# Normed rows as two fp16 parts and two more ring slots in an encoder layer with experts

## The chip, the cores and the metric

The kernel runs on one core of a Trainium2 chip. The metric is the device time of one execution in microseconds, the median of the runs. The core has five engines that are told apart here: PE (TensorE, matmuls; its weight loads are PEld), DVE (VectorE), ACT (ScalarE), POOL (GpSimd) and SP (SyncE), which issues most DMAs. A program line is written L123.

## The reference, cut to what matters

One layer for 512 tokens of 1024 features: three attention branches, gated and merged, a layer norm, then 16 experts, each of which picks its 64 best tokens, and a second layer norm. The expert part:

```
logits = x @ w_router;  aff = softmax(logits)               # (512, 16)
gate, idx = top_k(aff.T, 64)                                # each expert picks 64 tokens
xs = x[idx]                                                 # (16, 64, 1024)
h  = xs @ w_gate_up                                         # (16, 64, 2048), weights (16, 1024, 2048)
ye = (silu(h[..., :1024]) * h[..., 1024:]) @ w_down         # weights (16, 1024, 1024)
ffn = zeros.at[idx].add(ye * gate)
x = layer_norm(alpha * x + ffn)
```

Everything is float32. The expert weights are 16 x 12 MB, read once.

## The kernel before

**First half: attention.** 74 weight units of 128x1024 numbers come over the SP queue into `raw` (two buffers, tag "raw"; units 2 to 9 go in pairs into halves of larger tiles). `hi_lo` splits each one into a high part (ACT, L84) and a rest (DVE, L85), so that three matmuls give nearly the precision of float32. The high part rotates over three buffers of the tag "hi", the rest over two of "lo" and one of "lo2". Softmax results use two buffers each of the tags "P" and "PT". An order written by hand interleaves attention units (`Attn.step`) with the projections.

**Routing.** The last products (`w_half`, L991) use `mh` and `ml` (buffers G0a to G1b). Beside them the rows are normed (`x1_norm`): the normed row times X_SCALE is kept as a high part `XH` (4 bytes, buffers A5 and A6) and a rest `XL` (fp16, buffer A8, written by POOL at L960). DVE finds the threshold of each expert (`rounds`), and PE counts positions with `tri_t` (buffer VS) at L1081 and L1084; `pos` tells which slot a token takes.

**Experts.** They go in quarters of four. `onehot(qd)` compares positions with slot numbers on DVE (L1100) into a 4-byte one-hot matrix, and ACT casts it to fp16 (L1103). `gather(qd)` multiplies: for each of 8 column blocks, four matmuls of `XH` with the 4-byte one-hot (L1113) and four of `XL` with the fp16 one (L1115); then `aff2`, the affinities in two parts, is gathered into `gw` (L1130, L1135). `gate_up(e, ks)` needs one load per k, 128 rows of the gate/up weights (L1149), `down(e)` four loads per expert (L1182). `act_h` lies between them, `h_transpose` and `slots_T` turn operands, and `combine` adds expert pairs back into the token rows. The last expert's down product is done by column quarters (`last_down`, `product`, L1297), followed by the second norm and the stores.

**The ring.** All 192 expert loads, 1 MB each (8 KB a partition), stand in one fixed order in `Ring`: the first four gate/up loads of an expert, the four down loads of the expert before, the other four gate/up loads; at the end the down loads of the last two experts. The buffers are those that earlier stages leave:

```
RING = ("E0", "A2", "A3", "A0", "A1", "B0", "B1", "P", "PT", "A4", "raw", "G0a", "G0b", "A7", "G1a", "G1b", "lo", "Ma", "Mb",
        "X")
ONCE = ("G1a", "G1b", "lo")
PAIRED = {"raw": ("raw", "raw"), "P": ("P", "P"), "PT": ("PT", "PT"), "lo": ("lo", "lo"), "X": ("VS", "lo2")}
N_EARLY = 11
```

Buffers of `ONCE` serve one load and then go to other uses. A load into a `PAIRED` buffer is issued as two DMAs of half the size (L754), each of 4 KB a partition; into any other as one (L756). A down load takes two rows of 4 KB from the weights for each partition; the last expert's (L750) take pieces of 1 KB. SP issues in program order and waits before an issue until the buffer is free. The first 10 loads go out beside the last weight units (hooks in `after`), then come `ring.upto(N_EARLY + 2)` and, after the routing, `ring.upto(len(RING))`; from there on `ring.done`, called after each load's last matmul, lets the next one go.

Of the kernel before, what the change touches and what calls it, by code (L numbers as in the profile page):

```python
# [18 lines left out]
P = 128  # L19
# [21 lines left out]
def layer_kernel(ctx: ExitStack, tc: tile.TileContext, xt, xn, memt, wu, bgate, rpb, gains, wrt,  # L41
# [62 lines left out]


    class Stream:
# [9 lines left out]
        def _dma(self):  # L116
            i = self.nd
            if 2 <= i < 10:
                if i % 2 == 0:
                    self.wide = R(("A7", "A8", "B0", "B1")[i // 2 - 1], [P, 2, 1024], f"raw{i}")  # L120
                t = self.wide[:, i % 2]
            else:
                t = R("raw", [P, 1024], f"raw{i}", bufs=2)  # L123
            nc.sync.dma_start(t, wu[i])
            self.raw[i] = t
            self.nd += 1
            for f in after.pop(i, ()):
                f()

        def _split(self):  # L130
            i = self.ns
            if i >= self.nd:
                self._dma()
            raw = self.raw.pop(i)
            if i == N_UNITS - 1:
                both = R("A7", [P, 2, 1024], "wlast", F32R)
                hi, lo = both[:, 0], both[:, 1]
            else:
                hi = R("hi", [P, 1024], f"whi{i}", F32R, bufs=3)
# [30 lines left out]
    raw0 = R("raw", [P, 1024], "raw0", bufs=2)  # L170
    hi0 = R("hi", [P, 1024], "whi0", F32R, bufs=3)
# [33 lines left out]
    csn_t = cp.tile([P, NT, 2, 32], F32, name="csn_t")  # L205
    nc.sync.dma_start(csn_t, csn)
    gain_t = cp.tile([P, 2, 64], F32, name="gain_t")
    nc.sync.dma_start(gain_t, bass.AP(tensor=gains.tensor, offset=gains.offset, ap=[[0, P], [64, 2], [1, 64]]))
    nc.gpsimd.tensor_scalar(gain_t[:, 0], gain_t[:, 0], 0.125, None, op0=ALU.mult)
    mask_t = cp.tile([P, 3, 32], F32, name="mask_t")  # L210
    nc.sync.dma_start(mask_t, nmask)
    bg_t = cp.tile([P, 24], F32, name="bg_t")
# [272 lines left out]
    class MemUnit:  # L485
# [9 lines left out]
        def soft(self):  # L495
            self.p = R("P", [P, 2, 256], f"mp{self.hp}{self.m}", bufs=2)
# [15 lines left out]
        def tev(self):  # L512
            self.pt = R("PT", [P, 4, P], f"mpt{self.hp}{self.m}", bufs=2)
            nc.vector.tensor_copy(self.pt, self.t)
# [14 lines left out]
    class GqaUnit:  # L529
# [14 lines left out]
        def soft(self):  # L544
            self.p = R("P", [P, 2, S], f"gp{self.hp}{self.m}", bufs=2)
# [18 lines left out]
        def tev(self):  # L564
            self.pt = R("PT", [P, 2, 4, P], f"gpt{self.hp}{self.m}", bufs=2)
            nc.vector.tensor_copy(self.pt[:, 0], self.t[0])
            nc.scalar.copy(self.pt[:, 1], self.t[1])
# [32 lines left out]
    class NaUnit:  # L600
# [17 lines left out]
        def soft(self):  # L618
            self.p = R("P", [P, 2, 2, 256], f"np{self.id}", bufs=2)
# [24 lines left out]
        def tev(self):  # L644
            self.pt = R("PT", [P, 2, 4, P], f"npt{self.id}", bufs=2)
# [69 lines left out]
    class Ring:  # L715
# [15 lines left out]
        def load(self):  # L731
# [10 lines left out]
            if kind == "gu":  # L742
                src = wgu[e, k * P:(k + 1) * P, :].rearrange("p (j n) -> p j n", j=2)
            elif e < NEXP - 1:
                src = wdn[e, k * 256:(k + 1) * 256, :].rearrange("(j p) n -> p j n", p=P)
            else:
                t = [x.rearrange("p (c n) -> p c n", c=4) for x in t]
                src = wdn[e, :, k * 256:(k + 1) * 256].rearrange("(j c p) n -> p j c n", p=P, c=4)
                for j in range(2):
                    nc.sync.dma_start(t[j], src[:, j])  # L750
                src = None
            if src is not None and tag in PAIRED:
                for j in range(2):
                    nc.sync.dma_start(t[j], src[:, j])  # L754
            elif src is not None:
                nc.sync.dma_start(full, src)  # L756
# [196 lines left out]
    def x1_norm(m):  # L953
# [4 lines left out]
        h = XH[m // 2][:, m % 2]  # L958
        nc.scalar.copy(h, x1(m))
        nc.gpsimd.tensor_tensor(XL[:, m], x1(m), h.bitcast(F32), op=ALU.subtract)  # L960

    XH = [R(t, [P, 2, D], f"x{t}", F32R) for t in ("A5", "A6")]
    XL = R("A8", [P, NT, D], "xlo", F16)
# [123 lines left out]
    aff2 = cp.tile([P, NT, NEXP, 2], F32R, name="aff2")  # L1087
# [5 lines left out]
    OH16 = {}  # L1093

    def onehot(qd):
        oh = R("hi", [P, NT, 256], f"oh{qd}", F32R, bufs=3)
        o16 = R("oh16", [P, NT, 256], f"ohl{qd}", F16)
        OH[qd], OH16[qd] = oh, o16
        for m in range(NT):
# [3 lines left out]
            nc.scalar.copy(o16[:, m], oh[:, m].bitcast(F32))  # L1103

    def gather(qd):
        oh, o16 = OH[qd], OH16[qd]
        xs = [R("hi", [P, 4, 256], f"xs{qd}{j}", bufs=3) for j in range(2)]
        XS[qd] = xs
        for f in range(KD):
            g = PB("mm", f"ga{qd}{f}")[:, :256]  # L1110
            c = slice(f * P, (f + 1) * P)
            for m in range(NT):
                nc.tensor.matmul(g, XH[m // 2][:, m % 2, c], oh[:, m], start=(m == 0), stop=False)  # L1113
            for m in range(NT):
                nc.tensor.matmul(g, XL[:, m, c], o16[:, m], start=False, stop=(m == NT - 1))  # L1115
# [6 lines left out]
        if qd == 0:  # L1122
            nc.scalar.activation(aff2[:, :, :, 0], aff, AF.Copy, scale=0.5)
            nc.vector.scalar_tensor_tensor(aff2[:, :, :, 1], aff, 0.5, aff2[:, :, :, 0].bitcast(F32), op0=ALU.mult,
                                           op1=ALU.subtract)
        GW[qd] = small([P, 4], "gw", bufs=2)
        for i in range(0, 4, 2):
            gp = PB("Y", f"gw{qd}{i}")
            for m in range(NT):
                nc.tensor.matmul(gp[:, 0:4], oh[:, m, i * CAP:(i + 2) * CAP],  # L1130
                                 aff2[:, m, 4 * qd + i:4 * qd + i + 2].rearrange("p e a -> p (e a)"),
                                 start=(m == 0), stop=(m == NT - 1))
            for j in range(2):
                for b in (0, 64):
                    nc.vector.tensor_reduce(GW[qd][b:b + 64, i + j:i + j + 1], gp[j * 64:j * 64 + 64, 2 * j:2 * j + 2],  # L1135
                                            axis=AX.X, op=ALU.add)

# [25 lines left out]
    def h_transpose(e):  # L1163
# [4 lines left out]
        t = R("hi", [P, 4, P], f"hT{e}", bufs=3) if e == NEXP - 1 else R("tmp", [P, 4, P], f"hT{e}", bufs=2)  # L1168
# [3 lines left out]
    def down(e, mid=lambda: None):  # L1172
# [14 lines left out]
        if ep == 0:  # L1187
            YP[pr] = (R("lo", [P, D], f"yh{pr}", F32R, bufs=2), R("lo", [P, D], f"yl{pr}", F32R, bufs=2))
# [31 lines left out]
    def residual():  # L1220
        for h in range(2):
            c = slice(h * 512, (h + 1) * 512)
            a = []
            for mp in range(2):
                acc_of(2 * mp)
                a.append(ACC[mp][:, :, c])
                nc.vector.tensor_tensor(a[mp], XH[mp][:, :, c].bitcast(F32), XL[:, 2 * mp:2 * mp + 2, c], op=ALU.add)
# [205 lines left out]
    for e in range(NEXP):  # L1433
# [31 lines left out]
        else:  # L1465
# [3 lines left out]
            g2 = R("hi", [P, D], "ln2g", bufs=3)  # L1469
# [19 lines left out]
def _perm(a):  # L1489
    return a.reshape(8, 8, 8, -1).swapaxes(0, 1).reshape(512, -1)  # L1490


def _prep(inp):
# [48 lines left out]
    for ty in range(3):  # L1542
# [21 lines left out]
        "wdn": np.asarray(inp["w_down"])[0],  # L1564
# [26 lines left out]
```

## Time and profile before

| | |
|---|---|
| median of 3 runs | 998.72 us (998.05 to 1001.01) |
| profiled execution | 997.83 us, span 995.9 us |
| PE busy | 955.8 us (96%) |
| PE weight loads | 631.3 us (63%) |
| DVE / ACT / POOL busy | 459.5 / 273.8 / 75.2 us |
| mean granted clock of PE | 0.988 |
| read from HBM | 247.84 MB, 251 GB/s over the span |

The page divides the span in 40 slices of 24.9 us; a digit there is the busy share in tenths. A row of a windows answer has the stretch and its length, then busy time and number of instructions of PE, PEld, DVE, ACT and POOL, then the granted clock, the mean busy share of the 16 DMA engines, and the GB/s that they moved. Packets can overlap a little, so a share slightly over 1 is a full DMA. A row of the chain that ended last, or of a timeline, has start and duration in microseconds, the engine (SPq is SP's queue), the line and the operation. A row of the waits has the total in microseconds, the number of times and the longest one. A row of a group has busy time and mean nanoseconds of one, then the idle time before.

### The profile page before, as it was taken

The numbers are of one execution on the slowest core, as the hardware profiler recorded it, in microseconds if no ns is written. First come the engines' busy times: TensorE is split into PE (matmuls) and PEld (weight loads), VectorE is DVE, ScalarE is ACT, GpSimd is POOL, SyncE is SP. The second block draws the span as 40 slices with busy tenths as digits, with TensorE's granted clock in tenths as the row PEclk, the third lists the DMA queues.
The fourth block names the chain that finished last, engine by engine and source line by source line (L and its number), as shares of the span: only waits on it lengthen the run. The fifth ranks groups of instructions, "written<-read, shape, count | busy, mean of one in ns | idle before, by whom it ended". The sixth has DMA issues, their size and how long they took to land.

```text
span 995.9 us, 13692 instructions
## 1 busy us (share of the span) xinstructions
PE 955.8 (96%) x5504; PEld 631.3 (63%) x5504; DVE 459.5 (46%) x897; ACT 273.8 (27%) x547; POOL 75.2 (8%) x77
## 2 busy tenths in 40 slices
PE   7999899999999999999968999999999999998998
PEld 7899787889888888889954334533353333432355
DVE  5437678664376566256582155331322222231327
ACT  5434345444354444333341010200020001100021
POOL 0002403000131231000040000000000000000002
PEclk9999999999999999999987999999999999999999
DMA  8221211111432332665448999999999999999992
GB/s 340 98 85 65 64 64 43 64 48 61 110 113 81 93 88 94 237 253 222 159 180 339 368 424 420 423 421 422 425 423 422 424 424 424 423 422 421 425 397 97
DMA packets 67422, 251.61 MB, mean 253 GB/s; under 512 B 14720, under 2 KB 19488, under 8 KB 54944
## 3 DMA queue, kind: packets, MB, share of 16 engines
q1 hardware_dynamic: 66784, 249.44, 64.1%
q10 hardware_dynamic: 576, 1.31, 0.3%
q8 instruction: 43, 0.70, 0.3%
q14 instruction: 19, 0.16, 0.0%
HBM read 247.84 MB, written 2.10 MB: 251 GB/s over the span
## 4 chain that ended last, share of the span: by engine, by line
PE 80%; DMA 9%; DVE 6%; ACT 2%; POOL 2%; issue 1%; SPq 0%; POOLq 0%; ACTq 0%
PE g L1149 10%; PE u L1149 9%; PE y L1182 8%; DMA gu<-in_wgu 5%; PE gate L231 4%; PE gate L233 4%; PE gate L232 4%; DMA dn<-in_wdn 3%; PE pr L231 2%; PE ga L1113 2%; PE pr L232 2%; PE pr L233 2%; PE cb L1249 2%; PE ga L1115 2%; PE nqk L233 1%; PE nqk L232 1%
## 5 line engine op out<-in xcount | busy, mean ns | idle before, releaser
L1149 PE MATMUL g<-gu,xs 128*64 128x512 f32 x512 | 134.6, 604 | 5.5 <-DMA gu<-in_wgu 5.4
L85 DVE TENSOR_TENSOR wlo<-raw,whi 128x1024 fp32r<-128x1024 f32 (+2 forms) x75 | 92.7, 1237 | 87.7 <-ACT whi L84 87.3
L1149 PE MATMUL u<-gu,xs 128*64 128x512 f32 x512 | 131.6, 592 | 0.2 <-DMA gu<-in_wgu 0.2
L1182 PE MATMUL y<-dn,hT 128*64 128x512 f32 x480 | 106.8, 594 | 2.4 <-DMA dn<-in_wdn 2.2
L84 ACT CAST yh<-y 64x512 fp32r<-64x512 f32 x30 | 17.4, 579 | 249.0 <-PE y L1182 221.1
L84 ACT CAST whi<-raw 128x1024 fp32r<-128x1024 f32 (+2 forms) x75 | 77.0, 1027 | 25.3 <-PE wo L979 9.4
L1149 PEld LDWEIGHTS u<-gu,xs 128*64 128x64 f32 x512 | 36.7, 137 | 73.6 <-issue 68.3
L85 DVE TENSOR_TENSOR yl<-y,yh 64x512 fp32r<-64x512 f32 x30 | 20.7, 689 | 135.7 <-ACT yh L84 125.1
L1182 PEld LDWEIGHTS y<-dn,hT 128*64 128x64 f32 x480 | 33.8, 137 | 72.1 <-issue 63.1
L1149 PEld LDWEIGHTS g<-gu,xs 128*64 128x64 f32 x512 | 31.3, 136 | 62.4 <-issue 43.9
L1252 DVE TENSOR_TENSOR acc<-acc,cb 128x512 f32<-128x512 f32 x56 | 35.4, 683 | 35.1 <-PE cb L1250 35.1
L1170 DVE COPY hT<-ht 128x512 f32<-128x512 f32 x16 | 11.0, 690 | 62.1 <-PE ht L1167 62.1
L1314 POOL TENSOR_TENSOR acc<-acc,ln2g 128x512 f32<-128x512 f32 x4 | 5.1, 1277 | 452.3 <-DVE l2s L1326 452.1
L231 PE MATMUL gate<-xha,whi 128*128 128x512 f32 x96 | 38.9, 406 | 0.0
L232 PE MATMUL gate<-xla,whi 128*128 128x512 f32 x96 | 37.5, 390 | 0.0
L233 PE MATMUL gate<-xha,wlo 128*128 128x512 f32 x96 | 37.5, 390 | 0.0
L233 PE MATMUL gate<-xhb,wlo 128*128 128x512 f32 x96 | 37.4, 389 | 0.0
L231 PE MATMUL gate<-xhb,whi 128*128 128x512 f32 x96 | 37.3, 389 | 0.0
L232 PE MATMUL gate<-xlb,whi 128*128 128x512 f32 x96 | 37.3, 389 | 0.0
L550 ACT ACTIVATE gp<-gs,nm 128x512 f32<-128x512 f32 x32 | 21.7, 683 | 52.3 <-DVE nm L549 52.3
L1159 ACT ACTIVATE tg<-g 128x512 f32<-128x512 f32 x16 | 9.6, 597 | 89.5 <-PE g L1149 89.5
L1160 DVE SCALAR_TENSOR_TENSOR tg<-tg,g 128x512 f32<-128x512 f32 x16 | 11.0, 685 | 38.7 <-ACT tg L1159 38.7
(382 smaller groups left out, 1990.3 us busy)
## 6 DMA issues: line engine op xcount, KB each, us to landing
gu<-in_wgu SPq DMA_DIRECT2D x95, 1024.0 KB
dn<-in_wdn SPq DMA_DIRECT2D x49, 1024.0 KB
raw<-in_wu SPq DMA_DIRECT2D x73, 512.0 KB
gu<-in_wgu SPq DMA_DIRECT2D x66, 512.0 KB
dn<-in_wdn SPq DMA_DIRECT2D x30, 512.0 KB
xr<-in_xt SPq DMA_DIRECT2D x4, 512.0 KB
x<-in_xn SPq DMA_DIRECT2D x2, 1024.0 KB
bf<-in_rpb SPq DMA_DIRECT2D x64, 24.0 KB
```

The costliest lines, as they stand in the source:

```text
L84: nc.scalar.copy(hi, src)
L85: nc.vector.tensor_tensor(lo, src, hi.bitcast(F32), op=ALU.subtract)
L231: nc.tensor.matmul(acc, w_h, rh[:, k], start=(k == 0), stop=False)
L232: nc.tensor.matmul(acc, w_h, rl[:, k], start=False, stop=False)
L233: nc.tensor.matmul(acc, w_l, rh[:, k], start=False, stop=(k == nk - 1))
L550: nc.scalar.activation(self.p[:, h], self.s[h], AF.Exp, bias=nm[:, h:h + 1], accum_out=self.sm[:, h:h + 1])
L1113: nc.tensor.matmul(g, XH[m // 2][:, m % 2, c], oh[:, m], start=(m == 0), stop=False)
L1115: nc.tensor.matmul(g, XL[:, m, c], o16[:, m], start=False, stop=(m == NT - 1))
L1149: nc.tensor.matmul(GU[e][b][hf * 64:hf * 64 + 64], xs, w[b][:, hf * 512:hf * 512 + 512], start=(k == 0), stop=(k == KD - 1))
L1182: nc.tensor.matmul(y[o * 64:o * 64 + 64], hT[:, c, hf * 64:hf * 64 + 64], w[j][:, o * 512:(o + 1) * 512], start=(k == 0 and j == 0), stop= ...
L1249: nc.tensor.matmul(cb, g[:, m], yh[:, c], start=True, stop=False)
L1252: nc.vector.tensor_tensor(a, a, cb, op=ALU.add)
```

## The change

The normed rows are kept as two fp16 parts (`XH` in A5, `XL` in A6, X_SCALE 1024), and the one-hot matrix in fp16 alone, in a buffer "oh" of its own, which held small constants (`csn_t`, `gain_t`, `mask_t`, `bg_t`) until then. The affinities are split into three fp16 parts (`split_aff`), and the gathered gates are scaled back on DVE. The slot transposes become matmuls with an fp16 identity.

The down weights are laid out on the host in the order of the slots, so that each partition of a load is one piece of 8 KB, those of the last expert too. `raw`, `lo`, `P` and `PT` become one tile of two halves each (`twin`), used in turn, so that the ring takes each as one buffer and one DMA. "hi" has two buffers and "hi3" the third. The ring gets the slots A8 and VS; X is made of lo2 and hi3 and stands ahead of Ma and Mb; N_EARLY is 12. `g2` moves to A5, the last `hT` to A6, and the pair of `yh` and `yl` into one tile.

```diff
-RING = ("E0", "A2", "A3", "A0", "A1", "B0", "B1", "P", "PT", "A4", "raw", "G0a", "G0b", "A7", "G1a", "G1b", "lo", "Ma", "Mb",
-        "X")
+RING = ("E0", "A2", "A3", "A0", "A1", "B0", "B1", "A8", "P", "PT", "A4", "raw", "G0a", "G0b", "A7", "G1a", "G1b", "lo", "X", "Ma", "Mb",
+        "VS")
 ONCE = ("G1a", "G1b", "lo")
-PAIRED = {"raw": ("raw", "raw"), "P": ("P", "P"), "PT": ("PT", "PT"), "lo": ("lo", "lo"), "X": ("VS", "lo2")}
-N_EARLY = 11
-X_SCALE = 8192.0
+PAIRED = {"X": ("lo2", "hi3")}
+N_EARLY = 12
+X_SCALE = 1024.0
+A_SCALE = 16384.0
...
+    twins = {}
+
+    def twin(tag, dt=F32):
+        if tag not in twins:
+            twins[tag] = [R(tag, [P, 2, 1024], f"{tag}_twin", dt), 0]
+        t = twins[tag]
+        t[1] += 1
+        return t[0][:, (t[1] - 1) % 2]
+
+    def hi_tile(i):
+        if i % 3 == 2:
+            return R("hi3", [P, 1024], f"whi{i}", F32R)
+        return R("hi", [P, 1024], f"whi{i}", F32R, bufs=2)
...
-                t = R("raw", [P, 1024], f"raw{i}", bufs=2)
+                t = twin("raw")
...
-        return R("lo", [P, 1024], f"wlo{i}", F32R, bufs=2)
+        return twin("lo", F32R)
...
-            self.p = R("P", [P, 2, S], f"gp{self.hp}{self.m}", bufs=2)
+            self.p = twin("P").rearrange("p (h c) -> p h c", h=2)
...
             tag = self.first[i] if i < nf else self.again[(i - nf) % len(self.again)]
+            if kind == "gu":
+                src = wgu[e, k * P:(k + 1) * P, :].rearrange("p (j n) -> p j n", j=2)
+            else:
+                src = wdn[e, k].rearrange("p (j n) -> p j n", j=2)
             if tag in PAIRED:
-                t = [R(g, [P, D], f"{kind}{e}_{k}_{j}", bufs=None if tag == "X" else 2)
-                     for j, g in enumerate(PAIRED[tag])]
+                t = [R(g, [P, D], f"{kind}{e}_{k}_{j}") for j, g in enumerate(PAIRED[tag])]
+                for j in range(2):
+                    nc.sync.dma_start(t[j], src[:, j])
             else:
                 full = R(tag, [P, 2, D], f"{kind}{e}_{k}")
                 t = [full[:, j] for j in range(2)]
-            if kind == "gu":
-                src = wgu[e, k * P:(k + 1) * P, :].rearrange("p (j n) -> p j n", j=2)
-            elif e < NEXP - 1:
-                src = wdn[e, k * 256:(k + 1) * 256, :].rearrange("(j p) n -> p j n", p=P)
-            else:
+                nc.sync.dma_start(full, src)
+            if kind == "dn" and e == NEXP - 1:
                 t = [x.rearrange("p (c n) -> p c n", c=4) for x in t]
-                src = wdn[e, :, k * 256:(k + 1) * 256].rearrange("(j c p) n -> p j c n", p=P, c=4)
...
-        h = XH[m // 2][:, m % 2]
-        nc.scalar.copy(h, x1(m))
-        nc.gpsimd.tensor_tensor(XL[:, m], x1(m), h.bitcast(F32), op=ALU.subtract)
-
-    XH = [R(t, [P, 2, D], f"x{t}", F32R) for t in ("A5", "A6")]
-    XL = R("A8", [P, NT, D], "xlo", F16)
+        nc.scalar.copy(XH[:, m], x1(m))
+        nc.gpsimd.tensor_tensor(XL[:, m], x1(m), XH[:, m], op=ALU.subtract)
+
+    XH, XL = (R(t, [P, NT, D], f"x{t}", F16) for t in ("A5", "A6"))
...
     def onehot(qd):
-        oh = R("hi", [P, NT, 256], f"oh{qd}", F32R, bufs=3)
-        o16 = R("oh16", [P, NT, 256], f"ohl{qd}", F16)
-        OH[qd], OH16[qd] = oh, o16
+        OH[qd] = oh = R("oh", [P, NT, 256], f"oh{qd}", F16)
...
-            nc.scalar.copy(o16[:, m], oh[:, m].bitcast(F32))
+
+    def split_aff():
+        a, b = (R("t", [P, NT * NEXP], n, bufs=2).rearrange("p (m e) -> p m e", m=NT) for n in ("affs", "affr"))
+        nc.scalar.activation(aff3[:, :, :, 0], aff, AF.Copy, scale=A_SCALE)
+        nc.vector.scalar_tensor_tensor(a, aff, A_SCALE, aff3[:, :, :, 0], op0=ALU.mult, op1=ALU.subtract)
+        nc.scalar.copy(aff3[:, :, :, 1], a)
+        nc.vector.scalar_tensor_tensor(aff3[:, :, :, 2], a, 1.0, aff3[:, :, :, 1], op0=ALU.mult, op1=ALU.subtract)
...
             for m in range(NT):
-                nc.tensor.matmul(g, XH[m // 2][:, m % 2, c], oh[:, m], start=(m == 0), stop=False)
+                nc.tensor.matmul(g, XH[:, m, c], oh[:, m], start=(m == 0), stop=False)
             for m in range(NT):
-                nc.tensor.matmul(g, XL[:, m, c], o16[:, m], start=False, stop=(m == NT - 1))
+                nc.tensor.matmul(g, XL[:, m, c], oh[:, m], start=False, stop=(m == NT - 1))
...
+        nc.vector.tensor_scalar(gw, gw, 0.5 / A_SCALE, None, op0=ALU.mult)
...
-            nc.tensor.transpose(gp[:, m], OH[qd][:, m, h * P:(h + 1) * P].bitcast(F32), ident)
+            nc.tensor.matmul(gp[:, m], OH[qd][:, m, h * P:(h + 1) * P], id16, start=True, stop=True)
...
+def _down_slots(w):
+    import numpy as np
+    a = w.reshape(NEXP, 4, 2, 128, 1024).swapaxes(2, 3).reshape(NEXP, 4, 128, 2048).copy()
+    a[-1] = w[-1].reshape(2, 4, 128, 4, 256).transpose(3, 2, 0, 1, 4).reshape(4, 128, 2048)
+    return a
```

More of the change, by code (lines that the diff above doesn't have):

```diff
@@ L138, in _split @@
             else:
-                hi = R("hi", [P, 1024], f"whi{i}", F32R, bufs=3)
+                hi = hi_tile(i)
                 lo = lo_tile(i)
@@ L169, in layer_kernel @@
     memr = R("A2", [P, KD, 256], "memr")
-    raw0 = R("raw", [P, 1024], "raw0", bufs=2)
-    hi0 = R("hi", [P, 1024], "whi0", F32R, bufs=3)
+    raw0 = twin("raw")
+    hi0 = hi_tile(0)
     lo0 = lo_tile(0)
@@ L495, in soft @@
         def soft(self):
-            self.p = R("P", [P, 2, 256], f"mp{self.hp}{self.m}", bufs=2)
+            self.p = twin("P")[:, :512].rearrange("p (h c) -> p h c", h=2)
             nm = small([P, 2], "nm")
@@ L512, in tev @@
         def tev(self):
-            self.pt = R("PT", [P, 4, P], f"mpt{self.hp}{self.m}", bufs=2)
+            self.pt = twin("PT")[:, :512].rearrange("p (k c) -> p k c", k=4)
             nc.vector.tensor_copy(self.pt, self.t)
@@ L618, in soft @@
         def soft(self):
-            self.p = R("P", [P, 2, 2, 256], f"np{self.id}", bufs=2)
+            self.p = twin("P").rearrange("p (h i c) -> p h i c", h=2, i=2)
             nm = small([P, 2, 2], "nm4")
@@ L644, in tev @@
         def tev(self):
-            self.pt = R("PT", [P, 2, 4, P], f"npt{self.id}", bufs=2)
+            self.pt = twin("PT").rearrange("p (h k c) -> p h k c", h=2, k=4)
             nc.vector.tensor_copy(self.pt[:, 0], self.t[0])
@@ L1122, in gather @@
         if qd == 0:
[L1123 to L1126, printed above, removed]
+            split_aff()
+        GW[qd] = gw = small([P, 4], "gw", bufs=2)
         for i in range(0, 4, 2):
@@ L1187, in down @@
         if ep == 0:
-            YP[pr] = (R("lo", [P, D], f"yh{pr}", F32R, bufs=2), R("lo", [P, D], f"yl{pr}", F32R, bufs=2))
+            both = R("lo", [P, 2, D], f"y{pr}", F32R)
+            YP[pr] = (both[:, 0], both[:, 1])
         yh, yl = YP[pr]
@@ L1468, in layer_kernel @@
             slots_T(e // 2)
-            g2 = R("hi", [P, D], "ln2g", bufs=3)
+            g2 = R("A5", [P, D], "ln2g")
             for h in range(2):
```

40 lines of the change are left out of this document (17 added, 23 removed).

## The prediction

> **What bounds the kernel now.** I read the slices of the page first, to see which stage is bound by what.
>
> ```profile
> PE   7999899999999999999968999999999999998998
> DMA  8221211111432332665448999999999999999992
> GB/s 340 98 85 65 64 64 43 64 48 61 110 113 81 93 88 94 237 253 222 159 180 339 368 424 420 423 421 422 425 423 422 424 424 424 423 422 421 425 397 97
> DMA packets 67422, 251.61 MB, mean 253 GB/s; under 512 B 14720, under 2 KB 19488, under 8 KB 54944
> ```
>
> Up to slice 20 (about 500 us) TensorE is busy and the DMA engines are not: that half is attention and its projections, bound by TensorE. In the second half, the experts, both rows show nines, and the bytes stand at 420 to 425 GB/s slice after slice. A busy PE is not a PE at its peak, so the two have to be told apart. Windows over the stretches do it.
>
> ```profile
> core 0: us, PE busy (x) PEld busy (x) DVE busy (x) ACT busy (x) POOL busy (x), PEclk, DMA share, GB/s
> 484.50:509.50 25.00, 24.45 (x204) 23.68 (x204) 16.65 (x87) 7.98 (x18) 5.83 (x6) 1.00 0.10 36
> 509.50:532.00 22.50, 9.22 (x74) 7.70 (x72) 16.46 (x65) 7.51 (x16) 5.73 (x6) 0.59 0.95 372
> 532.00:565.00 33.00, 32.15 (x166) 14.12 (x166) 5.26 (x16) 3.00 (x6) 0.00 (x0) 0.97 0.87 316
> 565.00:950.00 385.00, 374.35 (x1824) 150.04 (x1822) 112.50 (x192) 42.37 (x78) 0.00 (x0) 1.00 1.02 423
> 825.00:950.00 125.00, 116.15 (x570) 46.36 (x568) 30.20 (x59) 14.56 (x27) 0.00 (x0) 1.00 1.02 423
> ```
>
> From 565 to 950 the DMA share is 1.02: the DMA engines have no pause in 385 us. The weights that they bring, 16 experts with 12 loads of 1.05 MB each, are fixed, so the time at which the last down load lands is 565 plus the bytes that are left by then, over 423 GB/s. TensorE lives on the stock in the ring of load buffers until about 825: of those 260 us it loses 260 - (374.35 - 116.15) = 1.8. From 825 to 950 it loses 125 - 116.15 = 8.85 us. The chain that ended last shows what it loses them to:
>
> ```profile
> 825.52 17.60 DMA gu<-in_wgu
> 910.92 16.79 DMA gu<-in_wgu
> 946.51 16.01 DMA dn<-in_wdn
> 962.57 1.94 PE y L1182 x8
> ```
>
> Late in the experts the chain leaves TensorE and goes through loads, and the last one, issued at 946.51, releases the last down product of expert 14 at 962.57. What follows, 995.9 - 962.57 = 33.3 us, is a chain of matmuls, statistics and stores. So the end is: last down load of expert 14, plus 33.3 us. The stage before 565 decides how much is left to load; here is the queue that issues the loads:
>
> ```profile
> 474.36 0.43 SPq L756 DMA_DIRECT2D gu<-in_wgu  x1
> 482.82 1.46 SPq L754 DMA_DIRECT2D gu<-in_wgu  x2
> 509.57 0.33 SPq L756 DMA_DIRECT2D gu<-in_wgu  x1
> 511.01 1.93 SPq L756 DMA_DIRECT2D dn<-in_wdn  x4
> 512.98 1.17 SPq L754 DMA_DIRECT2D gu<-in_wgu  x2
> 514.25 8.49 SPq L756 DMA_DIRECT2D gu<-in_wgu  x2
> 527.75 0.80 SPq L754 DMA_DIRECT2D gu<-in_wgu  x2
> 536.47 9.29 SPq L756 DMA_DIRECT2D gu<-in_wgu  x4
> ```
>
> L756 issues a whole load of 1.05 MB, L754 one in two halves. After the load at 482.82 the queue stands until 509.57, when the buffers of `mh` come free, and the DMA engines move 36 GB/s in those 25 us. The loads up to 527.75 fill the rest of the ring (20 loads). From 536.47 four loads go out over 9.29 us, one each 3 us, as TensorE frees a slot: until 565 the loads are limited by slots (316 GB/s, share 0.87), and from 565 on by the DMA engines.
>
> **Two more ring slots.** A8 is eighth in the ring now, and VS is last; with the two, 22 loads are out before the first expert has freed anything, instead of 20. Of these A4's load, the eleventh, needs nothing that comes late, so it goes out right behind the load of 474.36 and lands in the idle stretch before 509.57: 25 us at 423 GB/s would hold 10 MB, it needs 1.05. The other one is VS. Its buffer holds `tri_t` until the count matmuls:
>
> ```profile
> SPq L754 <- PE cnp L1084: 5.0, 1, 5.0
> SPq L756 <- POOL xlo L960: 7.4, 1, 7.4
> ```
>
> This 5.0 us wait stands before the load of 527.75 today (buffers VS and lo2). In the changed order lo2 goes with hi3, ahead of Ma and Mb, and VS with its wait is last. Nothing is behind VS on SP's queue but the load into E0, which can't go out before 536.47 anyway, so the wait costs nothing; the DMA engines meanwhile have ten loads from 509.57 (10 x 1.05 / 0.423 = 24.8 us, to about 534) where they had nine. From then on to 565 each load waits for its slot, and with 22 slots the load that goes out at a given time is two further in the order. So at 565 two loads more have landed: 2.1 MB / 0.423 GB/us = 5.0 us off the end. Bounds: 2.5 us if VS's load collides with the refill and counts only later, 5.0 as the other end, since from 565 on the DMA engines are the limit; I take 5.0.
>
> **Pieces of 8 KB.** Of a down load each packet has 4 KB today, as have the halves of P, PT, raw and X; a whole gate/up load has 8 KB. What that is worth is read where one kind flows alone. These loads were issued:
>
> ```profile
> 901.75 4.44 SPq L756 DMA_DIRECT2D dn<-in_wdn  x4
> 910.92 13.52 SPq L756 DMA_DIRECT2D gu<-in_wgu  x7
> 942.53 4.35 SPq L756 DMA_DIRECT2D dn<-in_wdn  x4
> ```
>
> The chain has 16 to 17 us from an issue to the release of its reader, and a load takes 2.5 us of the stream. Counted back from the releases, with some 2 us for the last step, the first row's loads flow at about 911 to 921, gate/up loads of the second at 928 to 940, the third row's at 950 to 960:
>
> ```profile
> 910.90:920.80 9.90, 7.57 (x36) 2.16 (x33) 0.69 (x1) 0.00 (x0) 0.00 (x0) 1.00 1.02 420
> 928.30:940.50 12.20, 12.20 (x54) 5.02 (x52) 6.40 (x10) 0.60 (x1) 0.00 (x0) 1.00 1.01 424
> 950.50:960.40 9.90, 9.90 (x50) 3.37 (x46) 2.80 (x8) 2.08 (x3) 0.00 (x0) 1.00 1.02 417
> 841.40:851.10 9.70, 8.41 (x64) 6.08 (x60) 2.98 (x5) 1.93 (x4) 0.00 (x0) 1.00 1.01 427
> ```
>
> 4 KB pieces give 417 and 420, 8 KB pieces 424 and 427 (the last row: the four whole gate/up loads behind the one that the chain has at 825.52). With the change only X, one load in 19, is in 4 KB pieces; the stage's mean goes from 423 to about 425.7: 385 x (1 - 423/425.7) = 2.4 us. Ends: 0 if some other ceiling holds the mean at 423, 3.6 if all run at 427. I take 2.5.
>
> The Trainium skill, page "DMA: Bandwidth & Descriptors", section "Why small descriptors are slow (HBM only)", puts about 3 cycles of 32 bytes on each packet: 131 cycles for 4 KB and 259 for 8 KB, 1.2% apart. The rows above are 1.7% apart, the same direction; by the page alone, with half of the bytes in 4 KB pieces, the estimate would be 385 x 0.6% = 2.2 us.
>
> The last expert's down loads, in 1 KB pieces today and in 8 KB pieces then, lie beside the products of the last 33 us. I count 0.5 us for all that starts earlier there (ends 0 and 1).
>
> **TensorE's side.** Without any wait for loads it could come at most 8.85 us earlier, and 0.85 of these are its own: an earlier stretch with a gather in it and no late load has that gap too, 25 - 24.15 us. So 8 us can be taken, unless it gets rid of work as well, and it does:
>
> ```profile
> 725.00:750.00 25.00, 24.15 (x146) 12.96 (x144) 7.50 (x20) 6.01 (x12) 0.00 (x0) 1.00 1.02 423
> 536.43 0.67 PE ga L1113 x4
> 537.10 0.45 PE ga L1115 x4
> L1113 PE MATMUL ga<-oh,xA 128*128 128x256 f32 x128 | 25.0, 320 | 1.1 <-DVE oh L1100 1.1
> L1115 PE MATMUL ga<-ohl,xlo 128*128 128x256 f16 x128 | 20.6, 286 | 0.0
> L1103 ACT CAST ohl<-oh 128x256 f16<-128x256 f32 x16 | 5.6, 405 | 10.4 <-DVE oh L1100 10.4
> ```
>
> A column block of the gather takes 0.67 us for four matmuls with 4-byte operands, 0.45 for four with fp16. With both in fp16 at most 0.22 us x 8 per quarter is saved, 1.8 us; by the sums of the groups (25.0 against 20.6) 4.4 us over all four quarters, about 1.1 each. The slot transposes and gate products change likewise, by less. Two or three us of these come before the last experts; they are worth nothing where the loads are the limit, but they keep TensorE from becoming it. ACT loses 16 casts of 405 ns and gains one 128x128 copy; the split of `aff` has two steps more on ACT and DVE, and each quarter one more small DVE scaling of `gw`. Cover: TensorE is in gate_up meanwhile; uncovered it would be some 0.5 us, once, at the first gather. The first matmul of the gather waits for the one-hot compare, as before, so the start of the experts at 534 stays.
>
> Sum against the profiled execution, 997.83 us (span 995.9 and 1.9 around it): 5.0 + 2.5 + 0.5 = 8.0 us less, 989.8. The median shown, 998.72, is 0.9 above the profiled run; less the same 8.0 it is **990.7 us**.
>
> **The rivals.**
>
> First, *only the slots count*. Some ceiling other than the packets holds the stream at 423, and the time is 5 to 5.5 us less, 993.5. For it: 8 KB stretches give 424 at the lower, hardly over the mean. Against it: both 4 KB stretches lie under every slice of the mixed stage. The Trainium skill, in "DMA: Bandwidth & Descriptors", section "Where 436 GB/s comes from", names the core's share of HBM, about 358 GB/s, as what binds a load from HBM, which would make the piece size idle. The trace's 423 is above that, so the rule doesn't hold on this one busy core.
>
> Second, *the halves of a twin tile aren't told apart* (the other side). `raw`, `lo`, `P` and `PT` were two buffers each and are now the two halves of one tile that is never given back. If a write into one half waited for the readers of the other, the double buffering of the first 500 us would be gone. The price is the split of a weight unit:
>
> ```profile
> L85 DVE TENSOR_TENSOR wlo<-raw,whi 128x1024 fp32r<-128x1024 f32 (+2 forms) x75 | 92.7, 1237 | 87.7 <-ACT whi L84 87.3
> L84 ACT CAST whi<-raw 128x1024 fp32r<-128x1024 f32 (+2 forms) x75 | 77.0, 1027 | 25.3 <-PE wo L979 9.4
> ```
>
> One unit in three of the 74 writes a half of `lo` straight after the other, and TensorE would stand for the DVE step, 25 x 1.2 = 30 us; the 32 softmax steps at about as much could add 30 more. That gives 1029 to 1060. It decides from the first stall of over a microsecond per unit. Against it stands:
>
> ```profile
> 3.52 3.90 SPq L124 DMA_DIRECT2D raw<-in_wu  x5
> ```
>
> Five loads leave within 3.9 us, among them raw2 and raw3, and raw4 and raw5, which are halves of one tile each already; a load takes longer than that to land (2.5 us for twice the size at the stage's best, plus the way), and none has waited for its other half.
>
> Third, *TensorE is the limit after all*: its losses are 8 us, but if they came from single late loads and not from the rate, taking two slots more would remove only the first of them, and the end would come some 2 us earlier: 996.7. For it: TensorE's rows show nines, and it waits for nothing before 825. Against it: the DMA share is 1.02 over the whole stretch from 565, so the lag at 946.51 is the sum of all bytes, not one late load.
>
> **How the numbers follow.** About 0.3%, 3 us, is what a measurement of this kernel can tell from no change. The forecast (slots and pieces, 6 to 11 us less) has 0.65; only the slots 0.20; the third rival, or an even smaller gain, 0.07; the twins 0.08. The first two are faster by over 3 us: 0.85. Same: 0.07. Slower: 0.08. The range reaches from 986.5 (all upper ends, 5.0 + 3.6 + 1, and TensorE's saved work, 2.5) to 995 (2.5 from the slots and 1 from the pieces); the twins and the third rival stay outside.
>
> **What would show it.** Right: the idle stretch before 509 us has one load more; the stage from 565 on moves about 425 to 426 GB/s with almost no packets under 8 KB; the last quarter of expert 14's down product, today released at 962.57, comes at about 954.5; TensorE's losses after 825 shrink to 2 or 3 us. Wrong on the pieces: the stage stays at 423 and the end moves by 5. Wrong on the slots: the stretch to 565 ends with as many loads as before. If stretches before 480 us last longer than today, the twins were it.

## The result and the profile after

The changed kernel takes 994.64 us (median of 10 runs, 994.02 to 998.28); the kernel before takes 998.08 (median of 10, 996.83 to 1001.23). The ratio is 0.9965, 95% interval 0.9952 to 0.9977: 3.4 us faster, where 8.0 were predicted. The profiled execution after took 996.59 us, 994.8 of them span.

From the page of the changed kernel, the rate in 40 slices and the packets:

```profile
GB/s 338 100 77 74 64 52 55 64 43 65 83 120 100 95 80 86 232 275 212 212 160 407 401 419 421 419 422 419 420 421 420 421 421 421 420 421 420 421 332 85
DMA packets 52607, 251.61 MB, mean 253 GB/s; under 512 B 14113, under 2 KB 14785, under 8 KB 28993
```

The packets under 8 KB fell from 54944 to 28993, as the change says. But the slices of the second half stand at 419 to 422 GB/s, where before they had 420 to 425. Larger pieces, and the stream is slower. Windows over the stages say the same (the columns: stretch, its length, TensorE busy with its count, granted clock, share of the DMA engines, GB/s):

```profile
core 0: us, PE busy (x), PEclk, DMA share, GB/s
480.00:509.00 29.00, 28.46 (x240) 1.00 0.21 85
565.00:700.00 135.00, 134.14 (x672) 1.00 1.01 420
700.00:825.00 125.00, 124.23 (x606) 1.00 1.02 420
825.00:950.00 125.00, 115.26 (x572) 1.00 1.02 421
```

The first row is the idle stretch ahead of the experts. Before it moved 46 GB/s; 39 more over 29 us are 1.1 MB, one load, as predicted. The others should have read 425 to 426. The prediction's other sign for the slots lies between them, in the stretch to 565 us; the kernel before first, then the changed one:

```profile
534.00:565.00 31.00, 30.14 (x157) 1.00 0.86 310
534.00:565.00 31.00, 30.23 (x162) 1.00 1.00 392
```

The share of the DMA engines there went from 0.86 to 1.00: slots hold the loads up much less.

The end of the experts, on TensorE's timeline of the changed kernel:

```profile
957.07 1.94 PE L1192 MATMUL y<-dn,hT 128*64 128x512 f32 x8 [0.23 <-DMA dn<-in_wdn]
959.66 1.97 PE L1308 MATMUL yq<-dn,hT 128*64 128x128 f32 x32 [0.65 <-DMA dn<-in_wdn]
```

The last quarter of expert 14's down product is released at 957.07 instead of 962.57: 5.5 us earlier, not the 8 that would have made it 954.5. (By the prediction's own sum it should have been 955.1: 0.5 of the 8 us were put behind this release.) The first product of expert 15 then waits 0.65 us for its own load. After that every step keeps a lead of some 4.7 us, until the last low-rank and diagonal matmuls; from the chains of waits, the kernel before first, then the changed one:

```profile
986.42 0.96 PE lr L1393 x3
987.38 1.05 PE lr L1397 x2
989.32 1.05 PE lr L1397 x2
```

```profile
981.70 0.96 PE lr L1404 x3
982.66 1.51 PE lr L1408 x2
985.74 2.00 PE lr L1408 x2
```

The same two matmuls take 1.05 us in one and 2.00 in the other: TensorE's granted clock fell to half for the last 12 us of this execution (0.76 in the mean of 970 to 995), which costs 3.6 us of the 4.7. In most of the ten executions the span was 992.2 to 992.9, some 2 us less than in this one, so the median loses less there.

So two questions: why the larger pieces did not make the stream faster, and whether the tail took the gain.

### The profile page after: what moved, and what is told of

It reads as the page before. It is cut to its first block, busy times and chain, and to the rows that moved or that the text cites. A ratio compares the mean times of both kernels' runs of the same rounds, so it can differ in the third digit from the quotient of the medians.

```text
span 994.8 us, 13602 instructions
## 1 busy us (share of the span) xinstructions
PE 953.6 (96%) x5504; PEld 624.5 (63%) x5504; DVE 459.9 (46%) x902; ACT 268.7 (27%) x533; POOL 74.2 (7%) x77
## 2 busy tenths in 40 slices
DMA packets 52607, 251.61 MB, mean 253 GB/s; under 512 B 14113, under 2 KB 14785, under 8 KB 28993
## 4 chain that ended last, share of the span: by engine, by line
PE 73%; DMA 16%; DVE 6%; POOL 2%; ACT 2%; issue 1%; SPq 0%; POOLq 0%; ACTq 0%; DVEq 0%
DMA gu<-in_wgu 10%; PE g L1159 8%; PE u L1159 7%; PE y L1192 6%; DMA dn<-in_wdn 6%; PE gate L247 4%; PE gate L248 4%; PE gate L249 4%; PE pr L247 2%; PE pr L248 2%; PE pr L249 2%; PE ga L1124 2%; PE nqk L247 1%; PE nqk L249 1%; PE nqk L248 1%; PE ga L1126 1%
## 5 line engine op out<-in xcount | busy, mean ns | idle before, releaser
L85 ACT CAST y<-y 64x512 fp32r<-64x512 f32 x30 | 17.4, 579 | 249.5 <-PE y L1192 219.6
L86 DVE TENSOR_TENSOR y<-y,y 64x512 fp32r<-64x512 f32 x30 | 20.7, 689 | 138.1 <-ACT y L85 138.1
L86 DVE TENSOR_TENSOR lo_twin<-raw_twin,whi 128x1024 fp32r<-128x1024 f32 (+2 forms) x46 | 55.3, 1201 | 48.0 <-ACT whi L85 47.9
L85 ACT CAST whi<-raw_twin 128x1024 fp32r<-128x1024 f32 (+2 forms) x67 | 68.7, 1025 | 18.8 <-PE wo L986 9.4
L86 DVE TENSOR_TENSOR wlo<-raw_twin,whi 128x1024 fp32r<-128x1024 f32 x21 | 27.1, 1292 | 35.0 <-ACT whi L85 34.9
L248 PE MATMUL gate<-xla,whi 128*128 128x512 f32 x96 | 37.5, 391 | 0.0
L566 ACT ACTIVATE P_twin<-gs,nm 128x512 f32<-128x512 f32 x32 | 21.7, 683 | 52.4 <-DVE nm L565 52.4
L249 PE MATMUL gate<-xha,lo_twin 128*128 128x512 f32 x80 | 31.2, 390 | 0.0
L249 PE MATMUL gate<-xhb,lo_twin 128*128 128x512 f32 x80 | 31.1, 389 | 0.0
```

Source lines behind the costliest of these rows:

```text
L85: nc.scalar.copy(hi, src)
L86: nc.vector.tensor_tensor(lo, src, hi.bitcast(F32), op=ALU.subtract)
L248: nc.tensor.matmul(acc, w_h, rl[:, k], start=False, stop=False)
L249: nc.tensor.matmul(acc, w_l, rh[:, k], start=False, stop=(k == nk - 1))
L566: nc.scalar.activation(self.p[:, h], self.s[h], AF.Exp, bias=nm[:, h:h + 1], accum_out=self.sm[:, h:h + 1])
```

## The experiments

All but the last were timed against the kernel before in five rounds; ratios are to it, with 95% intervals. How long single DMA packets took, and how many bytes had landed by a time, comes from the DMA records of each trace.

### Back to 20 slots (e1)

```diff
 # the changed kernel
-RING = (..., "B1", "A8", "P", ..., "lo", "X", "Ma", "Mb", "VS")
+RING = (..., "B1", "P", ..., "lo", "Ma", "Mb", "X")
-N_EARLY = 12
+N_EARLY = 11
```

> The changed kernel with its ring back at 20 slots in the order of before (A8 and VS are taken out, X behind Ma and Mb, 11 early loads); the 8 KB pieces, the fp16 parts and the twins stay. Theory (the two slots are all of the gain, the pieces give nothing): the last quarter of expert 14's down product is released near 962.5 us again, as in the kernel before, instead of 957.07; the time is that of the kernel before within about 1 us, apart from what the last 20 us do with the clock (up to 4 us more). Rival (the pieces do their 2.5 us and something else in the changed kernel eats it): release near 960, loads landing every 2.46 us in the stream, time some 2.5 us under the kernel before.

1.0033 (1.0018 to 1.0047): slower than the kernel before by 3.3 us. The rival is out; the first theory left up to 4 us for the clock, so the time alone does not decide about it. The stream says more.

```profile
700.00:825.00 125.00, 122.13 (x592) 1.00 1.01 420
825.00:950.00 125.00, 111.53 (x543) 1.00 1.01 420
950.00:960.00 10.00, 10.00 (x40) 0.66 1.02 423
```

With the ring of before and pieces of 8 KB the stream runs at 420, under the 423 of before; TensorE loses 13 us in 825 to 950 (and its granted clock dips to 0.66 after 950, so the release is no good measure in this profile). Something else in the change takes away from the stream. Against the changed kernel the slots are worth 0.0068 of 998 us, 6.8 us (by the two intervals, 1.9 either way).

### All loads in 4 KB pieces (e2)

```diff
-  src = wgu[e, k * P:(k + 1) * P, :].rearrange("p (j n) -> p j n", j=2)
+  src = wgu[e, k].rearrange("j p n -> p j n")   # host: (e, k, j, p, n); the same for wdn
```

> The changed kernel with every gate/up and down load laid out in host memory so that it is moved in 4 KB pieces, nothing else. Theory (a ceiling on the stream other than the packets): loads land every 2.485 us as in the changed kernel, release of the last quarter of expert 14's down product at 957 within 1 us, same time as the changed kernel within 1 us. Rival (each piece costs time, as the prediction had it, 427 against 418 GB/s): a load every 2.50 to 2.51 us, over some 155 loads 3 to 4 us later against the changed kernel's 2.485, and up to 7 by the prediction's two rows.

1.0069 (1.0051 to 1.0088), some 10 us over the changed kernel.

```profile
565.00:700.00 135.00, 134.14 (x670) 1.00 1.03 409
825.00:950.00 125.00, 110.05 (x522) 1.00 1.03 409
```

My theory of a ceiling falls: halving the pieces takes the stream from 420 to 409. But the rival does not fit either: it had 7 us at the most. And the kernel before, half of its bytes in 4 KB pieces, had 423: a mixture ran faster than all 4 KB and than all 8 KB. The pieces cost time, and something that came with the change costs time too.

### The pieces alone (e3)

```diff
 # the kernel before, shortened
-  elif e < NEXP - 1:
-      src = wdn[e, k * 256:(k + 1) * 256, :].rearrange("(j p) n -> p j n", p=P)
+  else:
+      src = wdn[e, k].rearrange("p (j n) -> p j n", j=2)   # host: _down_slots
```

> The kernel before with the down weights laid out by slot alone (whole loads in 8 KB pieces, the last expert's too); its 20 slots, its two-form operands and its tiles stay. Theory (ceiling): no change, release of the last quarter of expert 14's down product at 962.6 within 1 us, time within 1 us of the kernel before. Rival (pieces): 2.0 to 2.5 us earlier, and the tail up to 0.5 more.

0.9997 (0.9983 to 1.0011): no difference in time that could be told. A gain of up to 1.7 us is inside the interval; the 2.0 to 2.5 of the rival are not. The stream did gain:

```profile
700.00:825.00 125.00, 124.15 (x598) 1.00 1.01 425
825.00:950.00 125.00, 117.12 (x576) 1.00 1.01 425
```

425 instead of 423, with three quarters of the bytes in 8 KB pieces. The same pieces run at 425 in the old kernel and at 420 in the changed one. What differs is visible in single packets. Between 600 and 940 us they took (ns):

```
                      4 KB packets            8 KB packets
before                159 (nearly all)        309 (nearly all)
pieces alone          159 (nearly all)        309 (nearly all)
after                 159 to 172, mean 162    309 to 325, mean 314
20 slots              159 to 172, mean 163    309 to 325, mean 314
all 4 KB              159 to 172, mean 164    -
```

In the first two nearly every packet takes the same time to the nanosecond; in the others they scatter upwards, by 1.5 to 3% in the mean. They do so as early as the first dense stretch of loads, when the same buffers hold other data: from 14 to 26 us 31% of the 4 KB packets of the changed kernel take 159 ns, where before 99.8% did. Between 30 and 300 us, where little is loaded, it is 79% against 78% before: no difference. Nor do they in every dense stretch: from 560 to 570 us, at 423 GB/s, 90% of its 8 KB packets still take 309 ns, and from 600 on some 10%. That points at where the tiles lie, not at what is done with them. The program's layout shows it: four constants (`csn_t`, `gain_t`, `mask_t`, `bg_t`, 2016 bytes) moved from ahead of the large tiles to a tile among them, and `aff2` gave way to `aff3` and `id16` (128 bytes more). Before, the first large tile begins at byte 10496 of a partition, a multiple of 256; after, at byte 8608, 160 beside one. All other large tiles follow in whole multiples of 512, so every ring slot is shifted alike.

### More filler at the end (e4)

`keep_warm(n)` issues n matmuls whose result nobody reads, to keep TensorE occupied.

```diff
-        keep_warm(18)
+        keep_warm(22)
...
-        keep_warm(2)
+        keep_warm(4)
```

> The changed kernel with more filler matmuls on TensorE at its end: 22 instead of 18 before the last statistics, 4 instead of 2 behind the row transposes; they fill the two idle stretches of 0.91 and 0.22 us. Theory (the changed kernel gives back 2 to 4 us in its last 20 us, because TensorE's clock falls to half at 983 in front of the last eight matmul pairs): the last diagonal pairs take 1.05 us each again instead of 2.0, and the time is 1.7 to 4 us under the changed kernel, 5 to 7 us under the kernel before. Rival (the half clock falls where it will, whatever TensorE does there): same time as the changed kernel within 0.7 us, or up to 0.5 more for the added matmuls.

0.9963 (0.9949 to 0.9976), median 994.95: as the changed kernel. The profiled execution has the last diagonal pairs at full clock,

```profile
983.06 1.06 PE lr L1408 x2
985.00 1.06 PE lr L1408 x2
986.48 1.05 PE lr L1408 x2
```

but others of the same kernel took up to 998.47 us, and the spread is that of the changed kernel. Filling the idle stretches did not change the times: the theory falls. The half clock at the end is a matter of the single execution, not a cost of the change; the kernel before shows the same split. Of the 29 executions that were timed beside e1 to e4, 15 took 997.0 to 999.5 us at a mean granted clock of 0.986 to 0.988, and 14 took 1000.2 to 1001.9 at 0.980 to 0.985. What sets it stays open.

### Slots at a multiple of 64 bytes (e5)

```diff
-    gT = cp.tile([P, KD], F32, name="gT")
+    gT = cp.tile([P, KD + 8], F32, name="gT")[:, :KD]
```

> The changed kernel with 32 bytes more in one small constant (gT), so that every ring slot and every other large tile behind it begins at a multiple of 64 bytes in SBUF again, as in the kernel before; in the changed kernel they all begin 32 bytes beside one. Theory (in the changed kernel the pieces are worth what was predicted, but the shift of 32 bytes makes each packet longer: 8 KB in 311 to 321 ns where the kernel before has 309): nearly all 8 KB packets at 309 ns, the stage from 565 us at 425 to 427 GB/s instead of 420, the last quarter of expert 14's down product released some 4.5 to 6 us earlier, near 952, time 4.5 to 6 us under the changed kernel, 989 to 990.5 (8 to 9.5 under the kernel before). Rival (the packets are slowed by something else that came with the change, or by a ceiling): 313 ns and 420 GB/s stay, same time as the changed kernel within 0.7 us.

0.9953 (0.9936 to 0.9971), median 995.21: nothing changed, and the 8 KB packets still scatter upwards from 309 ns, to 314 in the mean.

```profile
565.00:700.00 135.00, 134.14 (x670) 1.00 1.01 420
825.00:950.00 125.00, 114.89 (x554) 0.97 1.01 421
```

### The kernel before, shifted (e6, e7, e8)

The same edit in the kernel before.

> The kernel before with 32 bytes more in the same small constant, so that its large tiles begin 32 bytes beside a multiple of 64; nothing else. Theory (alignment): 8 KB packets from 309 to some 314 ns, 4 KB packets from 159 to some 163, the stage from 423 to about 416 GB/s, and the time 5 to 9 us over the kernel before. Rival (something else in the change slows the packets): no difference.

1.0079 (1.0057 to 1.0102), 7.9 us slower (5.7 to 10.2), by 32 bytes of a constant that nothing reads:

```profile
565.00:700.00 135.00, 134.05 (x662) 1.00 1.02 415
825.00:950.00 125.00, 112.46 (x534) 1.00 1.02 415
```

423 became 415, and the packets 163 and 315 ns in the mean. Where the slots lie does matter. Then e5 only chose too small a boundary: its slots began at 64 bytes beside a multiple of 128.

Two more kernels went with these, 20 slots and 4 KB pieces with the same 32 bytes.

> The changed kernel with 20 slots in the order of before, and aligned as in e5: the pieces and the fp16 parts without the slots. Theory (alignment): 5 to 6 us under the same kernel unaligned (e1, 1.0033 of before), so 2 to 3 us under the kernel before, the prediction's term for the pieces; against e5 it is 5 to 6 us longer, the term for the slots. Rival: as e1, 1.003 of before.

> The changed kernel, aligned as in e5, with all loads in 4 KB pieces: against e5 it gives what a piece costs by itself. Theory (a packet costs 159 ns for 4 KB and 309 for 8 KB, 9 ns above twice the rate): the stage at 418 to 420 GB/s, 4.5 to 7 us longer than e5, and some 8 to 10 us shorter than the same kernel unaligned (e2, 1.0069 of before). Rival (piece size costs only where the tiles are beside the boundary): within 1 us of e5.

1.0043 (1.0027 to 1.0059) and 1.0061 (1.004 to 1.0082): as e1 and e2, both expectations missed for the same reason as in e5.

### Slots as in the kernel before (e9)

```diff
-    lnT = cp.tile([P, 2, KD], F32, name="lnT")
+    lnT = small([P, 2, KD], "lnT", bufs=1)      # and so gT and dg: 160 bytes
```

> The changed kernel with three small constants (lnT, gT and dg, 160 bytes) moved behind the large tiles, so that every ring slot begins at 256 bytes beside a multiple of 512 again, exactly as in the kernel before, with no byte more in use; with e5 they began at 448. Theory (the 64 bytes of e5 were too coarse a boundary; what counts is a multiple of 128 or 256): 8 KB packets at 309 ns, the stage from 565 us at 425 to 427 GB/s, the last quarter of expert 14's down product released near 952, time 989 to 990.5 or 0.991 of the kernel before. Rival (the shift slows the kernel before, e6, but the changed kernel's packets are slow for another reason): 312 to 313 ns, 420 GB/s, 0.9955 of the kernel before as e5.

0.9925 (0.9904 to 0.9946), median 992.0: faster than both kernels. Nearly all packets take 159 and 309 ns again.

```profile
565.00:700.00 135.00, 134.14 (x670) 1.00 1.01 425
700.00:825.00 125.00, 124.23 (x606) 1.00 1.01 426
825.00:950.00 125.00, 118.31 (x590) 1.00 1.01 426
```

On TensorE's timeline the last two quarters of expert 14's down product are one group; the second half of it begins at 954.0, against the 954.5 of the prediction:

```profile
952.15 3.71 PE L1192 MATMUL y<-dn,hT 128*64 128x512 f32 x16
956.46 1.97 PE L1308 MATMUL yq<-dn,hT 128*64 128x128 f32 x32 [0.60 <-DMA dn<-in_wdn]
```

The rate and the packets are as expected. The release is not as early as this run's own expectation, 952, and the time is a little over the 989 to 990.5 expected, whose ratio, 0.991, lies in the interval. The six executions go from 989.18 us at a mean granted clock of 0.985 to 993.75 at 0.980.

### The slots and the pieces apart, aligned (e10, e11)

The kernels of e1 and e2 with the edit of e9.

> The kernel of e1 (20 slots in the order of before, pieces of 8 KB, fp16 parts), with the slots' places as in e9: the pieces without the slots. Theory (boundary): some 5 us under e1, that is 1.5 to 2.5 us under the kernel before, the prediction's term for the pieces, and 5 to 6 us over e9, its term for the slots. Rival: 1.003 to 1.004 of the kernel before, as e1 and e7.

> The kernel of e2 (all loads in 4 KB pieces, 22 slots), with the slots' places as in e9. Theory (boundary, and 9 ns for each packet by itself): 4 KB packets at 159 ns, the stage at 417 to 420 GB/s instead of 409, 4 to 8 us over e9 and 6 to 10 us under e2. Rival (boundary alone, pieces cost nothing): within 1 us of e9; rival (no boundary): as e2 and e8, 1.006 to 1.007 of the kernel before.

20 slots: 0.9976 (0.9961 to 0.9992), the stream at 425 and 426; 4 KB pieces: 0.997 (0.9954 to 0.9987), all stretches at 420:

```profile
565.00:700.00 135.00, 134.14 (x670) 1.00 1.01 425
825.00:950.00 125.00, 114.46 (x556) 0.99 1.01 426
```

```profile
565.00:700.00 135.00, 134.14 (x672) 1.00 1.02 420
825.00:950.00 125.00, 114.68 (x556) 0.98 1.03 420
```

The kernel without the slots is 2.4 us faster than the kernel before (0.8 to 3.9). That is the pieces and the fp16 parts together; no run has the fp16 parts alone, and the pieces alone gave 0.3 (e3, at most 1.7). The slots are worth 0.9976 - 0.9925 = 0.0051, 5.1 us (2.6 either way); all 4 KB instead of 8 KB costs 0.0045, 4.5 us (2.7 either way). Each is what its theory said. By the bytes that had landed at 565 us the slots are two loads, as predicted: 80.6 MB in e9, 78.7 in e10.

### The stream by itself (e12)

> Not the layer at all: ten times 40 loads of 1 MB from the gate/up weights into 20 slots, nothing computed, and zeros stored. By the tile's name: a to e in 8 KB pieces, beginning 0, 32, 64, 128 and 256 bytes beside a multiple of 512; f, g, h in 4 KB pieces at 0, 32 and 256; i and j in 2 KB pieces at 0 and 32. Theory (boundary): a and e at 309 ns a packet, b and c at 312 to 316, d the open one (309 if 128 is enough); f and h at 159, g at 163 to 164; i near 84, j near 89; rates 16 engines times the packet's bytes over these. Rival (the packets are slowed by work of the engines in SBUF, not by where the slot begins): all 8 KB packets alike at 309, all 4 KB packets at 159.

Windows inside each of the ten stretches, in the order a to j:

```profile
15.00:94.00 79.00, 1.00 1.01 427
114.00:193.00 79.00, 1.00 1.01 421
214.00:293.00 79.00, 1.00 1.01 422
314.00:392.00 78.00, 1.00 1.01 422
413.00:491.00 78.00, 1.00 1.01 427
511.00:590.00 79.00, 1.00 1.03 421
611.00:692.00 81.00, 1.00 1.02 410
713.00:792.00 79.00, 1.00 1.03 421
813.00:894.00 81.00, 1.00 1.05 409
916.00:1002.00 86.00, 1.00 1.04 387
```

Nothing computes here (one execution), and the two effects stand apart. 8 KB pieces on a multiple of 512 or 256 bytes: 427. Beginning 32, 64 or 128 bytes beside it: 421 to 422, the open case d among them, so 128 is not enough. 4 KB: 421 on the boundary (f, h), 410 beside it (g). 2 KB: 409 and 387. The packets on the boundary take 309, 159 and 84 ns for 8, 4 and 2 KB, which is 9 ns for each packet and 37.5 for each KB. The stream does not pay all of the 9 ns, for packets overlap (the DMA share is 1.01 to 1.05): 16 at a time would give 424, 412 and 390 GB/s, the rates that were expected, and 427, 421 and 409 were measured. By these rates a packet more costs its engine about 4.5 ns. And 8 KB beside the boundary run as fast as 4 KB on it, 421: a rate that stands still can look like a ceiling and be two costs that match.

## Why the prediction was wrong

**Slots: right.** 5.0 us predicted; one load more in the idle stretch, two by 565 us (e9 against e10), and 5.1 us by the times of these two. Between the changed kernel and e1, both beside the boundary, it was 6.8. The release that came 5.5 us earlier can't be put down to the slots alone: it has the faster gathers and the slower stream in it too.

**Pieces: right for the stream, and given back by a term that the sum lacked.** The step "Pieces of 8 KB" took the rates of the kernel before, 424 and 427 against 417 and 420, and got 2.5 us. With the slots where that kernel has them the stage ran at 425 to 426, as written. In time, e10 gained 2.4 us with the fp16 parts in it, e3 without them at most 1.7, and half of the 4.5 us between e11 and e9 (the kernel before had half of its bytes in 4 KB pieces) is 2.2: the size is borne out roughly, not to the 0.1. The failed step is the silent one in front of it: that rates read from the old slots hold for the new ones. I listed the fp16 casts, copies and waits of the change and passed over the four constants that it moves, since they cost no instruction. They shift every slot off its boundary, and the 8 KB packets go from 309 to 314 ns in the mean. Some 390 us of stream at 420 instead of 425.5 GB/s are 5 us; by the times it is 0.9965 - 0.9925 = 0.0040, 4.0 us (2.5 either way). With the slots on their boundary the change is worth 7.5 us (0.9925) of the 8.0 predicted; without it 3.4 were left.

The Trainium skill, page "DMA: Bandwidth & Descriptors", section "How a descriptor splits into AXI transactions", has this boundary: a transaction starts at a multiple of 256 bytes, and what lies ahead of an unaligned start is fetched and not used. The stream agrees on the 256 (32, 64 and 128 are slow, 256 is not). An estimate from the page: 128 bytes add four beats of 32 to the 256 of an 8 KB piece, 1.6%, and 32 bytes add one, 0.4%. The stream lost 1.2 to 1.4% in rate, and a little more with 32 bytes (421) than with 128 (422), so the boundary agrees and the dependence on the distance does not. The page speaks of bytes that are fetched; here the side that begins beside the boundary is the one written, so what makes these packets longer stays open. I had read its neighbour, "Why small descriptors are slow (HBM only)", whose 3 cycles a packet gave the prediction's estimate of 1.2% between 4 and 8 KB; the stream by itself shows 421 against 427, 1.4%, so that rule came close here.

**The rivals.** "Only the slots count" came near in time (993.5), by luck: it said "some other ceiling", and there was none, for e2 and e9 move the stream to 409 and to 426. The halves of the twin tiles are told apart: the experts start at 533.91 us against 534.50 (rows below), so the first half did not lose the 30 us and more of that rival.

**Last expert and tail, 0.5 us: not seen.** Its first product waits 0.65 us for its load in the changed kernel and 0.60 in e9, where before it did not wait: the last loads come with the stream, not ahead of it. The half clock of the last 12 us stands in the profiles of the changed kernel and of e9; in that of e4 only the last 1.3 us have it, and in that of e1 it fell near 950 instead. It comes and goes, cost 3.6 us in the profile of the changed kernel, and had no term in the sum. The times above carry it, and with it part of their wide intervals.

**TensorE: more work saved, fewer waits removed.** From the first gate/up product to that release, the kernel before, the changed one, and e9:

```profile
534.50:962.57 428.07, 416.49 (x2033) 1.00 1.01 414
533.91:957.07 423.16, 410.80 (x2033) 1.00 1.01 418
535.08:953.92 418.84, 409.76 (x2034) 1.00 1.01 421
```

As many matmuls, 2033 or 2034, keep TensorE busy 5.7 us less (6.7 in e9), against the 4.4 of the gather groups in the prediction. It waits 12.4 us after, 11.6 before, 9.1 in e9. After 825, where the prediction had 2 or 3 us of its 8.85 left, TensorE loses 9.7 in the changed kernel and 6.7 in e9. So its losses did not shrink as written, not even with the rate that was predicted: much of what TensorE saved became waiting for loads. The third rival, TensorE as the limit, was further off than I had it.

## What to carry to other kernels

When an edit moves, shrinks or adds any tile, small ones too, look at where the tiles behind it begin: in this kernel, bound by its loads, slots that begin 160 bytes beside a multiple of 256 undid half of the change. Rates read from a trace hold for the places of that trace; list the layout among the things that a change moves. And when a stream settles on one rate, look at how long single packets take: packets that are all alike and packets that scatter tell a cost in the packets from a ceiling above them. Look in a long dense stretch; in the light stretches of this kernel the shifted packets looked like the others.

## What the hardware showed

In the long dense streams, into slots that begin 32, 64 or 128 bytes beside a multiple of 256 bytes, an 8 KB packet takes about 5 ns more (309 to 314). With 32 bytes a 4 KB packet takes 4 more (159 to 163), and so does a 2 KB one (84 to 88). In the weights' array the pieces begin at multiples of 2 KB in every one of these cases. Where little is loaded the difference does not show (79% of 4 KB packets at 159 ns against 78%), and what brings it on in a dense stretch is open. In the kernel before, that shift alone costs 7.9 us of 998.6. A packet's record has 9 ns that do not depend on its size from 2 to 8 KB, of which the stream pays about half. On this one busy core the stream reached 427 GB/s over 79 us.
